# A trunk layer in fp32 on one core: second tokens turned and weighted by ScalarE before the first products, last stores from two queues

## The chip, the core and the metric

The kernel runs on one core of a Trainium2 chip. A core has TensorE for products (PE in the profile, with PEld for its weight loads), VectorE (DVE), ScalarE (ACT), GpSimd (POOL) and SyncE (SP), which here only starts transfers. Each engine works through its own list of instructions in order, and waits on semaphores for the others. Transfers between the chip's main memory and the core's memory run on 16 DMA engines, which are fed by queues that SP, ACT and POOL fill. The metric is the device time of one execution in microseconds (us).

## What is computed

One decoder layer on 512 tokens of 1024 channels, all in fp32: a first RMSNorm and a wide projection, a convolution branch, gated linear attention, a merge with an output projection, a feed-forward block and a last RMSNorm. The change touches the start and the very end:

```python
u = _rmsnorm(h, norm1_g[l])
proj = u @ w_in[l]
a_glu, q, k, v, r, g_low, gate_a, gate_b = _split_cols(proj)
...
return _rmsnorm(h, final_g)
```

where `_rmsnorm(x, g)` is `x * rsqrt(mean(x*x) + EPS) * g`, over the channels of a token. The first thing the kernel produces is the first half (512 columns) of `v`, and the last is the final norm.

## The kernel before

**Products.** An fp32 product is made of three products in a format with fewer bits: each operand is split into a high part (`whi`, `uh`, or the first of two tiles named `h`) and a low part (`wlo`, `ul`, the second tile `h`), and low x high, high x low and high x high are added up in one bank. ScalarE makes the high part by a cast (L256 for weights, L469 for tokens), VectorE the low part by a subtraction (L259, L470). So a block of weights costs one ScalarE and one VectorE pass over 128x1024 elements, and then serves many products.

**The start.** The 512 tokens are four groups t = 0 to 3 of 128. Tokens arrive with a token in each row, and the products need a channel in each row, so TensorE turns each group by eight 128x128 transposes against an identity (`turn`, L378 to L380), four into each of two banks g = 0 and 1 (channels 0 to 511 and 512 to 1023). The weights of `v`'s first half come in four blocks `w_v` j = 0 to 3 of 256 channels each; block j serves channels k = 2j and 2j+1 (in units of 128).

Groups 0 and 1 don't wait for their norm. Their turned tokens are multiplied by the channel weights `norm1_g` alone (`gained`, L475, one VectorE pass over 512 columns from the bank), split (`split_plain`, L480), and used; the factor of each token is applied to the result when it leaves its bank (`v_done`, L534), and later to the kept tokens (`renormed`, L484). Groups 2 and 3 are normed first: `rms` (L452: two squares with sums on ScalarE, one VectorE instruction, one power on GpSimd), `shrunk` (L462, VectorE), then turned, then weighted and split by `spread_gain` (L382), whose high parts are eight ScalarE instructions over 128 columns each (L389: copy with a scale per row, read from the bank).

The transfers of the start are all issued by SP, in this order: x of group 0, `w_v` block 0, x of group 1, blocks 1 and 2, x of group 2, block 3, x of group 3 in two halves. Until the first tokens are there, TensorE multiplies ones by ones (`raise_clock`, L439): seven times before the first transposes and three times after them.

The start runs under a schedule written by hand (`start`, L422): TensorE, ScalarE, VectorE and SP keep the order in which the code calls them (L542 to L584). What matters here:

- TensorE: transposes of group 0; three warm products; four products of block 0 for group 0 that need no `wlo`; transposes of group 1, g = 0; the two products with `wlo`; transposes of group 1, g = 1; six products of block 0 for group 1, whose first needs the low part of group 1; blocks 1 and 2 for both groups; transposes of group 2; block 3; and so on.
- ScalarE: cast of group 0 g 0; cast of block 0; cast of group 1 g 0; cast of block 1; cast of group 0 g 1; cast of group 1 g 1; cast of block 2; squares of group 2; cast of block 3; squares of group 3 and so on.
- VectorE: weighting and low part of group 0 g 0; low part of block 0; weighting and low part of group 1 g 0; weighting of group 0 g 1; low part of block 1; low part of group 0 g 1; weighting and low part of group 1 g 1; low part of block 2; norm of group 2; low part of block 3.

`v_block(j, *ts, low_last, between)` (L509) issues the six products of block j for each group in `ts`; with `low_last` the two that need `wlo` come last, and `between` is called ahead of them.

**The end.** The last feed-forward product adds to the residual `hres`, and the class `Finish` (L1117) norms each group of tokens. For the last group, `store` (L1147) scales columns 0 to 383 on ScalarE (L1152) and columns 384 to 1023 on VectorE (L1155), and sends each part by its own transfer. Both transfers are issued by SP: L1157 (640 columns) and L1154 (384 columns). Three engines keep their written order there (`END`).

Of the kernel before, what the change touches and what calls it, by code (L numbers as in the profile page):

```python
# [14 lines left out]
AF = mybir.ActivationFunctionType  # L15
ALU = mybir.AluOpType

P = 128
D = 1024
T = 512  # L20
NT = T // P
KT = D // P
# [45 lines left out]
def trunk_layer(ctx: ExitStack, tc: tile.TileContext, a: dict, out: bass.AP):  # L68
    nc = tc.nc
# [23 lines left out]
    def nm(s):  # L93
        return f"{s}_{next(names)}"

    def heap(dt=F32):
        return hp.tile([P, T], dt, tag="h", name=nm("h"))
# [13 lines left out]
    def mm_bank():  # L111
        return ps.tile([P, T], F32, tag="mm", name=nm("mm"), bufs=5)

    def ax_bank():
        return ps.tile([P, T], F32, tag="ax", name=nm("ax"), bufs=3)
# [8 lines left out]
    gains = cp.tile([P, 2 * KT], F32, name="gains")  # L124
# [143 lines left out]
    def weight(name, j, ahead=LOOK):  # L268
        assert order[used[0]] == (name, j)
        prefetch(1)  # L270
        used[0] += 1
        prefetch(ahead)
        fill(RATE)
        return ready[used[0] - 1]
# [22 lines left out]
    def mm3(acc, l, r, first, last, more=False):  # L297

        (lh, ll), (rh, rl) = l, r
        kw = {"skip_group_check": True} if more else {}  # L300
        nc.tensor.matmul(acc, ll, rh, start=first, stop=False, **kw)  # L301
        nc.tensor.matmul(acc, lh, rl, start=False, stop=False, **kw)  # L302
        nc.tensor.matmul(acc, lh, rh, start=False, stop=last, **kw)  # L303
# [74 lines left out]
    def turn(x, banks, g):  # L378
        for k in range(4):
            nc.tensor.transpose(banks[g][:, k * P : (k + 1) * P], x[g][:, k * P : (k + 1) * P], ident)  # L380
# [29 lines left out]
    xs = {}  # L410
# [11 lines left out]
    start = tc.manual_schedule(engines=START)  # L422
# [21 lines left out]
    banks = {0: [ax_bank(), ax_bank()]}  # L444
# [7 lines left out]
    def rms(t):  # L452
        ss = small(2, "ss")
        for j in range(2):
            nc.scalar.activation(junk(T), xs[t][j], AF.Square, scale=1.0 / 32.0, accum_out=ss[:, j : j + 1])
        v = small(1, "var")
        nc.vector.scalar_tensor_tensor(v, ss[:, 0:1], EPS, ss[:, 1:2], ALU.add, ALU.add)
        return rsqrt(v, 1)
# [7 lines left out]
    unscaled = {}  # L466

    def split_by(f, hi, lo):
        nc.scalar.copy(hi, f)  # L469
        nc.vector.tensor_tensor(lo, f, hi.bitcast(F32), ALU.subtract)  # L470

    def by_token(x):
        return x.rearrange("p (k t) -> p k t", t=P)

    def gained(t, g):  # L475
        f = unscaled[t, g] = heap()
        gain = gains[:, g * 4 : g * 4 + 4].unsqueeze(2).to_broadcast([P, 4, P])
        nc.vector.tensor_tensor(by_token(f), by_token(banks[t][g]), gain, ALU.mult)

    def split_plain(t, g):  # L480
        plain[t, g] = (heap(F32R), heap(F32R))
        split_by(unscaled[t, g], *plain[t, g])
# [14 lines left out]
    def tokens(t):  # L497
        def normed(k):
            return tuple(x[:, t * P : (t + 1) * P] for x in acts1[k])

        return normed

    def as_landed(t):
        return lambda k: tuple(x[:, k % 4 * P : (k % 4 + 1) * P] for x in plain[t, k // 4])

    accs = [mm_bank() for _ in range(NT)]
    ws = []

    def v_block(j, *ts, low_last=False, between=None):  # L509
        for t in ts:  # L510
            src = as_landed(t) if t < 2 else tokens(t)
            last = []
            for i in range(2):
                k = 2 * j + i
                c = slice(i * T, (i + 1) * T)
                w = (ws[j][0][:, c], ws[j][1][:, c])
                if low_last:
                    ah, al = src(k)
                    nc.tensor.matmul(accs[t], al, w[0], start=k == 0, stop=False)
                    nc.tensor.matmul(accs[t], ah, w[0], start=False, stop=False)  # L520
                    last.append((ah, w[1]))
                else:
                    mm3(accs[t], src(k), w, k == 0, k == KT - 1)
            if between:
                between()
            for ah, wl in last:
                nc.tensor.matmul(accs[t], ah, wl, start=False, stop=False)

    def block_ready():
        ws.append(weight("w_v", len(ws), 0))  # L530
# [11 lines left out]
    banks[1] = [ax_bank(), mm_bank()]  # L542
    gained(0, 0)
    split_plain(0, 0)
    block_ready()
    v_block(0, 0, low_last=True, between=lambda: turn(xs[1], banks[1], 0))
    turn(xs[1], banks[1], 1)
    gained(1, 0)
    split_plain(1, 0)
    gained(0, 1)  # L550
    v_block(0, 1)
    block_ready()
    split_plain(0, 1)
    gained(1, 1)
    v_block(1, 0, 1, low_last=True)
    split_plain(1, 1)
    block_ready()
    v_block(2, 0, 1, low_last=True)
    r1[2] = rms(2)
    shrunk(2)  # L560
    banks[2] = turned(xs[2])
# [44 lines left out]
    for k in range(KT):  # L606
# [4 lines left out]
        c = heap()  # L611
# [95 lines left out]
    rows = slice(32, 32 + RANK)  # L707
# [9 lines left out]
    rows = slice(96, 96 + RANK)  # L717
# [374 lines left out]
    def first_of_pair(i, accs):  # L1092

        w = fp.tile([P, 3 * H], F32, tag="w", name=nm("w"), bufs=2)
        glu(i, accs, w[:, :T])
        nc.vector.tensor_tensor(w[:, T:], w[:, :H], w[:, H:T], ALU.subtract)
        y = fsplit(w.rearrange("p (c t) -> p c t", t=H)[:, 0:3:2, :], T, "y")
        return w, {"a11": y(0), "n3": y(1)}
# [18 lines left out]
    class Finish:  # L1117
# [29 lines left out]
        def store(self):  # L1147
            rows = slice(self.t * P, (self.t + 1) * P)
            if self.y:
                cut = T if self.t < NT - 1 else D - SPLIT  # L1150
                lo, hi = self.y[:, :cut], self.y[:, cut:]
                nc.scalar.activation(lo, lo, AF.Copy, scale=self.r)  # L1152
                if self.t == NT - 1:
                    nc.sync.dma_start(out[rows, :cut], lo)  # L1154
                nc.vector.tensor_scalar(hi, hi, self.r, None, ALU.mult)  # L1155
                if self.t == NT - 1:
                    nc.sync.dma_start(out[rows, cut:], hi)  # L1157
                else:
                    nc.sync.dma_start(out[rows, :], self.y)
                return  # L1160
            for n, y in reversed(self.parts):
                nc.scalar.activation(y, y, AF.Copy, scale=self.r)
                nc.sync.dma_start(out[rows, n * T : (n + 1) * T], y)
# [22 lines left out]
    for gi, pairs in enumerate(GROUPS):  # L1186
        acts = []
        early = {}
        if gi == 0:

            ws = [weight("w_up", j, 0) for i in pairs[0] for j in (i, FT + i)]
            accs = [mm_bank() for _ in ws]
# [7 lines left out]
        def both(i):  # L1200
            return early.get(i) or [col_tile(weight("w_up", i), acts2), col_tile(weight("w_up", FT + i), acts2)]

        for p, q in pairs:
            w, found = first_of_pair(p, both(p))
# [95 lines left out]
```

## Time and profile before

| | |
|---|---|
| time before, median of 3 runs | 841.06 us (840.03 to 841.2) |
| time of the profiled execution | 841.11 us |
| its span from first to last instruction | 839.4 us |
| TensorE's granted clock over the span | 0.997 |
| PE, DVE, ACT, POOL busy | 827.9, 649.8, 398.1, 41.8 us |

The profile has a page with shares and groups of instructions, and a trace that can be asked for more: instructions in order of time, waits (who waited for whom, in total, how often, and the longest), busy time in chosen stretches, and transfers with their time from issue to landing. A row of the timeline reads: start, duration, engine, line, operation, output<-inputs, shape, count, and in brackets the idle time before it and what ended it. L12 is line 12 of the kernel before, as printed above.

### The profile page before, as it was taken

How to read it: one execution, taken by the hardware profiler on the slowest of the kernel's cores; microseconds unless marked ns; L12 is line 12 of the kernel's file. 1: busy time of each engine (PE TensorE's matmuls, PEld its weight loads, DVE VectorE, ACT ScalarE, POOL GpSimd, SP SyncE). 2: the span in 40 equal slices, each digit the busy share in tenths (PEclk: the TensorE clock that was granted, in tenths of full speed). 3: DMA queues.
4: the chain of work that ended last, by engine and by line, in shares of the span. 5: the costliest groups of instructions: out<-in, count | busy, mean ns of one | idle time of the engine just before them, and what ended most of it. 6: DMA issues, size and time to landing. Idle time of an engine off the chain costs nothing.

```text
span 839.4 us, 10105 instructions
## 1 busy us (share of the span) xinstructions
PE 827.9 (99%) x3841; PEld 690.7 (82%) x3841; DVE 649.8 (77%) x954; ACT 398.1 (47%) x590; POOL 41.8 (5%) x64
## 2 busy tenths in 40 slices
PE   8999999999999999999999999999999999999996
PEld 6888888888888888888888898888888888888885
DVE  5779879999997798744687758778757777677795
ACT  5723337535443422449434766444434443444454
POOL 1000000000100100000001000000100010000111
PEclk9999999999999999999999999999999999999998
DMA  7333232222322322222346643335742249222462
GB/s 286 110 102 104 90 105 80 97 101 76 101 76 76 126 90 89 97 86 91 101 100 183 193 151 126 101 87 115 212 144 85 73 86 285 95 89 98 102 126 100
DMA packets 28465, 97.27 MB, mean 116 GB/s; under 512 B 3232, under 2 KB 3504, under 8 KB 28416
## 3 DMA queue, kind: packets, MB, share of 16 engines
q1 hardware_dynamic: 24928, 84.82, 30.0%
q0 software_dynamic: 3456, 11.80, 8.3%
q8 instruction: 30, 0.49, 0.2%
q14 instruction: 19, 0.16, 0.1%
q10 hardware_dynamic: 32, 0.01, 0.0%
HBM read 94.51 MB, written 2.10 MB: 115 GB/s over the span
## 4 chain that ended last, share of the span: by engine, by line
PE 92%; DVE 3%; ACT 2%; issue 1%; DMA 1%; POOL 0%; SPq 0%; POOLq 0%; DVEq 0%; ACTq 0%
PE mm L301 28%; PE mm L303 28%; PE mm L302 28%; DVE wlo L241 1%; DMA hres<-in_x_dram 1%; PE ax L845 1%; PE ax L380 1%; PE ax L847 1%; PE ax L827 1%; PE ax L303 1%; PE ax L301 1%; PE ax L302 1%; DVE wlo L259 1%; DVE hres L995 1%; PE ax L814 0%
## 5 line engine op out<-in xcount | busy, mean ns | idle before, releaser
L301 PE MATMUL mm<-uh,wlo 128*128 128x512 f32 (+1 forms) x768 | 294.7, 384 | 0.0
L303 PE MATMUL mm<-uh,whi 128*128 128x512 f32 (+1 forms) x768 | 292.2, 380 | 0.0
L302 PE MATMUL mm<-ul,whi 128*128 128x512 f32 (+1 forms) x768 | 292.0, 380 | 0.0
L256 ACT CAST whi<-raw 128x1024 fp32r<-128x1024 f32 x116 | 120.9, 1048 | 126.3 <-PE mm L303 94.8
L259 DVE TENSOR_TENSOR wlo<-raw,whi 128x1024 fp32r<-128x1024 f32 x116 | 141.1, 1219 | 34.8 <-ACT whi L256 34.5
L303 PEld LDWEIGHTS mm<-uh,whi 128*128 128x128 f32 x768 | 144.4, 188 | 27.8
L302 PEld LDWEIGHTS mm<-ul,whi 128*128 128x128 f32 x768 | 144.5, 188 | 27.4
L301 PEld LDWEIGHTS mm<-uh,wlo 128*128 128x128 f32 x768 | 144.5, 188 | 26.9
L604 DVE SCALAR_TENSOR_TENSOR c<-h,pp,c 128x511 f32<-128x511 f32 (+14 forms) x240 | 162.5, 730 | 0.7
L1075 DVE SCALAR_TENSOR_TENSOR tmp<-mm,pp,tmp 128x511 f32<-128x511 f32 x88 | 65.8, 748 | 66.7 <-ACT tmp L1073 65.6
L1073 ACT ACTIVATE tmp<-mm,pp 128x512 f32<-128x512 f32 x44 | 34.3, 779 | 61.5 <-PE mm L303 61.5
L240 ACT CAST whi<-kept 128x1024 fp32r<-128x1024 f32 (+1 forms) x32 | 31.7, 993 | 25.9 <-DVE kept L220 12.2
L241 DVE TENSOR_TENSOR wlo<-kept,whi 128x1024 fp32r<-128x1024 f32 (+1 forms) x32 | 36.7, 1153 | 4.3 <-ACT whi L240 4.1
L995 DVE TENSOR_TENSOR hres<-hres,mm 128x512 f32<-128x512 f32 (+1 forms) x49 | 32.6, 672 | 7.2 <-PE mm L303 3.9
L240 ACT CAST whi<-raw 128x1024 fp32r<-128x1024 f32 (+1 forms) x24 | 23.7, 995 | 17.0 <-PE mm L303 16.9
L241 DVE TENSOR_TENSOR wlo<-raw,whi 128x1024 fp32r<-128x1024 f32 (+1 forms) x24 | 27.3, 1153 | 1.6 <-ACT whi L240 1.6
L302 PE MATMUL mm<-wlo,sh 128*128 128x512 f32 x66 | 25.8, 391 | 0.0
L303 PE MATMUL mm<-whi,sh 128*128 128x512 f32 x66 | 25.7, 390 | 0.0
L301 PE MATMUL mm<-whi,sl 128*128 128x512 f32 x66 | 25.5, 389 | 0.0
L301 PE MATMUL mm<-h,wlo 128*128 128x512 f32 x64 | 25.4, 397 | 0.0
L349 POOL TENSOR_TENSOR rstd<-var,mhalf 128x1 f32<-128x1 f32 (+1 forms) x16 | 13.3, 840 | 241.4 <-DVE var L852 196.6
L303 PE MATMUL mm<-h,whi 128*128 128x512 f32 x64 | 24.9, 390 | 0.0
(253 smaller groups left out, 1148.7 us busy)
## 6 DMA issues: line engine op xcount, KB each, us to landing
raw<-in_w_up_dram SPq DMA_DIRECT2D x44, 512.0 KB, 3.5
raw<-in_w_glu_dram SPq DMA_DIRECT2D x16, 512.0 KB, 3.4
raw<-in_w_down_dram SPq DMA_DIRECT2D x15, 512.0 KB, 3.4
kept<-in_w_down_dram POOLq DMA_DIRECT2D x10, 512.0 KB, 5.5
raw<-in_w_v_dram SPq DMA_DIRECT2D x8, 512.0 KB, 4.0
raw<-in_w_qk_dram SPq DMA_DIRECT2D x8, 512.0 KB, 3.3
raw<-in_w_r_dram SPq DMA_DIRECT2D x8, 512.0 KB, 3.2
raw<-in_w_gb_dram SPq DMA_DIRECT2D x8, 512.0 KB, 3.3
```

What stands on the lines that cost most here:

```text
L240: nc.scalar.copy(hi, raw)
L241: nc.vector.tensor_tensor(lo, raw, hi.bitcast(F32), ALU.subtract)
L256: nc.scalar.copy(hi, raw)
L259: pace[0] = nc.vector.tensor_tensor(lo, raw, hi.bitcast(F32), ALU.subtract)
L301: nc.tensor.matmul(acc, ll, rh, start=first, stop=False, **kw)
L302: nc.tensor.matmul(acc, lh, rl, start=False, stop=False, **kw)
L303: nc.tensor.matmul(acc, lh, rh, start=False, stop=last, **kw)
L349: nc.gpsimd.tensor_tensor(r, v, mhalf[:, :n], ALU.pow)
L604: nc.vector.scalar_tensor_tensor(y[:, s:], c[:, : T - s], w, y[:, s:], ALU.mult, ALU.add)
L995: nc.vector.tensor_tensor(hres[t, n][:, c], hres[t, n][:, c], x[:, c], op)
L1073: nc.scalar.activation(z, acc, AF.Identity, bias=pp[:, PP_FB + m : PP_FB + m + 1], scale=w[2])
L1075: nc.vector.scalar_tensor_tensor(z[:, s:], acc[:, : T - s], w[j], z[:, s:], ALU.mult, ALU.add)
```

## The change

Four things change, and nothing else.

1. The four transposes of group 1, g = 0, stand ahead of all products of block 0 rather than between them.
2. For group 1 the channel weights are applied by ScalarE in four instructions of 128 columns (`gained_by_act`) in place of one VectorE instruction of 512 columns, for g = 0 and for g = 1. On ScalarE, the four for g = 0 stand between the cast of block 0 and the cast of group 1; those for g = 1 stand behind the cast of group 0 g 1.
3. The six products of block 0 for group 1 begin with the four that take the group's high part, and end with the two that take its low part. On VectorE the weighting of group 0 g 1 comes ahead of the low part of group 1 g 0. In blocks 0 to 2 for the other cases the order is low, high with `whi`, then high with `wlo`, each for both channels; block 3 and groups 2 and 3 keep their order.
4. In `store`, the transfer of columns 0 to 383 of the last group is issued by ScalarE rather than by SP.

```diff
+    def gained_by_act(t, g):
+        f = unscaled[t, g] = heap()
+        for k in range(4):
+            c = slice(k * P, (k + 1) * P)
+            nc.scalar.activation(f[:, c], banks[t][g][:, c], AF.Copy, scale=gains[:, g * 4 + k : g * 4 + k + 1])
...
+    LOW_LAST = ((1, 0), (0, 0), (0, 1))
+    HIGH_FIRST = ((0, 0), (0, 1), (1, 0))
+    ALL = ((1, 0), (0, 1), (0, 0))
+
+    def v_block(j, *ts, parts=None):
         for t in ts:
             src = as_landed(t) if t < 2 else tokens(t)
...
+            ks = (2 * j, 2 * j + 1)
+            todo = [(k, p) for p in parts for k in ks] if parts else [(k, p) for k in ks for p in ALL]
+            for n, (k, p) in enumerate(todo):
+                product(t, j, k, src, *p, j == 0 and n == 0, j == KT // 2 - 1 and n == len(todo) - 1)
+
+    def product(t, j, k, src, a_low, w_low, first, last):
+        w = ws[j][w_low][:, (k % 2) * T : (k % 2 + 1) * T]
+        nc.tensor.matmul(accs[t], src(k)[a_low], w, start=first, stop=last)
...
     gained(0, 0)
     split_plain(0, 0)
     block_ready()
-    v_block(0, 0, low_last=True, between=lambda: turn(xs[1], banks[1], 0))
+    turn(xs[1], banks[1], 0)
+    v_block(0, 0, parts=LOW_LAST)
+    gained_by_act(1, 0)
+    gained(0, 1)
+    split_plain(1, 0)
     turn(xs[1], banks[1], 1)
-    gained(1, 0)
-    split_plain(1, 0)
-    gained(0, 1)
-    v_block(0, 1)
+    v_block(0, 1, parts=HIGH_FIRST)
     block_ready()
     split_plain(0, 1)
-    gained(1, 1)
-    v_block(1, 0, 1, low_last=True)
+    gained_by_act(1, 1)
+    v_block(1, 0, 1, parts=LOW_LAST)
     split_plain(1, 1)
     block_ready()
-    v_block(2, 0, 1, low_last=True)
+    v_block(2, 0, 1, parts=LOW_LAST)
...
                 if self.t == NT - 1:
-                    nc.sync.dma_start(out[rows, :cut], lo)
+                    nc.scalar.dma_start(out[rows, :cut], lo)
```

From the transposes of group 2 on, every engine's list holds the same instructions in the same order as before, up to the last store.

More of the change, by code (lines that the diff above doesn't have):

```diff
@@ L507, in trunk_layer @@
     ws = []
-    def v_block(j, *ts, low_last=False, between=None):
+    LOW_LAST = ((1, 0), (0, 0), (0, 1))
+    HIGH_FIRST = ((0, 0), (0, 1), (1, 0))
+    ALL = ((1, 0), (0, 1), (0, 0))
+    def v_block(j, *ts, parts=None):
         for t in ts:
             src = as_landed(t) if t < 2 else tokens(t)
[L512 to L527, printed above, removed]
+            ks = (2 * j, 2 * j + 1)
[5 more added lines that the diff above has]
+        nc.tensor.matmul(accs[t], src(k)[a_low], w, start=first, stop=last)
     def block_ready():
```

## The prediction

> **What bounds the kernel now.** I read the page first, then TensorE's waits, the busy time by stretch, and the timeline of the start and of the end.
>
> ```profile
> span 839.4 us, 10105 instructions
> PE 827.9 (99%) x3841; PEld 690.7 (82%) x3841; DVE 649.8 (77%) x954; ACT 398.1 (47%) x590; POOL 41.8 (5%) x64
> PE 92%; DVE 3%; ACT 2%; issue 1%; DMA 1%; POOL 0%; SPq 0%; POOLq 0%; DVEq 0%; ACTq 0%
> ```
>
> TensorE is busy for 99% of the span and is 92% of the chain of waits, so a change that leaves its products as they are can only win where it waits. The waits (who for whom: us in total, times, longest) and the stretches (length, then busy time of PE first):
>
> ```profile
> PE mm L519 <- ACT whi L256: 1.3, 1, 1.3
> PE mm L301 <- DVE h L470: 1.3, 1, 1.3
> PE ax L380 <- ACT un L400: 0.3, 1, 0.3
> PE ax L302 <- DVE wlo L241: 0.3, 1, 0.3
> ...
> PEld mm L527 <- DVE wlo L259: 0.5, 1, 0.5
> ```
>
> ```profile
> 24.00:430.00 406.00, 406.00 (x1860) 338.23 (x1861) 336.46 (x503) 186.13 (x273) 10.19 (x12) 1.00 0.29 94
> 500.00:830.00 330.00, 330.00 (x1497) 274.68 (x1496) 245.07 (x327) 154.18 (x198) 17.48 (x22) 1.00 0.43 119
> ```
>
> The large waits are two of 1.3 us on lines of the start; between 24 and 430 us and between 500 and 830 us PE has no gap. So the start sets when an unbroken run of products begins, and what is won there should reach the end undiminished. Now the start, in order of time:
>
> ```profile
> 7.04 1.04 ACT L256 CAST whi<-raw 128x1024 fp32r<-128x1024 f32 x1
> 8.11 1.23 DVE L259 TENSOR_TENSOR wlo<-raw,whi 128x1024 fp32r<-128x1024 f32 x1 [0.25 <-ACT whi L256]
> 8.13 0.50 PE L519 MATMUL mm<-whi,h 128*128 128x512 f32 x1 [1.30 <-ACT whi L256]
> 9.18 0.60 PE L380 MATMUL ax<-ident,x 128*128 128x128 f32 x4
> 9.53 0.71 PE L527 MATMUL mm<-wlo,h 128*128 128x512 f32 x2
> 10.08 0.60 PE L380 MATMUL mm<-ident,x 128*128 128x128 f32 x4
> 10.54 0.62 ACT L469 CAST h<-h 128x512 fp32r<-128x512 f32 x1 [2.46 <-DVE h L478]
> 11.06 1.04 ACT L256 CAST whi<-raw 128x1024 fp32r<-128x1024 f32 x1
> 11.94 0.50 PE L301 MATMUL mm<-whi,h 128*128 128x512 f32 x1 [1.26 <-DVE h L470]
> 12.27 0.40 PE L302 MATMUL mm<-wlo,h 128*128 128x512 f32 x1
> ...
> 15.38 1.04 ACT L256 CAST whi<-raw 128x1024 fp32r<-128x1024 f32 x1
> 16.32 0.63 ACT L455 ACTIVATE junk<-x 128x512 bf16<-128x512 f32 x1
> 16.47 0.50 PE L519 MATMUL mm<-whi,h 128*128 128x512 f32 x1
> 17.73 0.73 PE L527 MATMUL mm<-wlo,h 128*128 128x512 f32 x2
> 18.67 0.88 DVE L464 TENSOR_SCALAR x<-x,rstd 128x512 f32<-128x512 f32 x2 [0.68 <-POOL rstd L349]
> 19.46 1.22 DVE L259 TENSOR_TENSOR wlo<-raw,whi 128x1024 fp32r<-128x1024 f32 x1
> 19.69 1.03 PE L380 MATMUL ax<-ident,x 128*128 128x128 f32 x8
> ```
>
> Three holes. At 11.94 PE waits for group 1's low part, which waits for the cast at 10.54, for VectorE's weighting, and for transposes that stood behind four products. At 16.47 it waits for the high part of block 2, at 17.73 for its low part; that cast starts at 15.38 only because ScalarE idled (2.46 us ahead of 10.54) and each cast behind it came late.
>
> **Prices.** A product after a wait takes 0.34 us to the next (11.94 to 12.27), else 0.23 (eight from 17.73 to 19.69, less 0.11 for the restart). Four transposes delay what follows by 0.35 (9.18 to 9.53). ScalarE begins an instruction 0.1 before the end of the one ahead (16.32 against 15.38 + 1.04).
>
> The trace has no ScalarE weighting with an fp32 result; the nearest rows read the same kind of bank with the same scale and write the high format, as the page of groups and as the timeline give it:
>
> ```profile
> L389 ACT ACTIVATE uh<-ax,gains 128x128 fp32r<-128x128 f32 x16 | 4.3, 379 | 0.0
> ...
> 21.53 2.16 ACT L389 ACTIVATE uh<-ax,gains 128x128 fp32r<-128x128 f32 x8
> ```
>
> Eight overlap: (2.16 - 0.38) / 7 = 0.25 from one to the next, so four take 3 x 0.25 + 0.38 = 1.13. That is my price; the upper bound is no overlap, 4 x 0.38 = 1.52, and there is no reason for less than 0.25.
>
> **The new order, step by step.** The moved transposes follow the last warm products, in a time when PE idles, if x of group 1 is there:
>
> ```profile
> 1.71 0.42 SPq L416 DMA_DIRECT2D x<-in_x_dram  x1
> x<-in_x_dram SPq DMA_DIRECT2D x1, 512.0 KB, 5.0
> ...
> 5.99 0.83 PE L441 MATMUL ax<-ones 128*128 128x128 f32 x6
> ```
>
> It lands at 1.71 + 5.0 = 6.71, as the warm products end (6.8). The transposes are done by 7.3, before the 8.13 at which products can start; they cost nothing, and would cost from a landing at 7.7 on.
>
> ScalarE: block 0's cast ends at 8.08. Weightings 7.98 to 9.12, cast of group 1 9.15 to 9.77, cast of block 1 9.68 to 10.72 (11.06 before), cast of group 0 g 1 10.63 to 11.25, weightings 11.16 to 12.30, cast 12.33 to 12.95, cast of block 2 12.86 to 13.90, where it began at 15.38 before: 2.5 us earlier although ScalarE has gained 2.3 us of work, for its waits go. Everything behind it there (squares of group 2, cast of block 3) moves by 2.5 as well, if the data are there; x of group 2, issued after block 2, landed by 10.5:
>
> ```profile
> 3.21 0.47 SPq L416 DMA_DIRECT2D x<-in_x_dram  x1
> x<-in_x_dram SPq DMA_DIRECT2D x1, 512.0 KB, 7.3
> ```
>
> TensorE: four products from 8.13 to 9.18 as before; then `wlo`, ready at 8.11 + 1.23 = 9.34, is a new wait of 0.2 (the transposes used to cover it). Two products 9.39 to 9.96, transposes g 1, and at 10.31 group 1's first product, whose high part has been ready since 9.77. Its low part is needed at 11.3; VectorE, rid of two weightings, makes it from 9.9 to 10.6. Six products end at 11.78, block 1's twelve at 14.52 (`whi` at 10.72, `wlo` at 11.97), block 2's at 17.26: its `whi` comes at 13.90, its `wlo` at 15.2 and is needed at 15.4. Group 2's transposes start at 17.26 rather than 19.69; their tokens are normed by 18.67 - 2.5 + 0.88 = 17.05. Block 3's `wlo` follows at 18.2 and is needed at 18.4.
>
> By holes: 1.6 at group 1's first product (11.94 to 10.31; of it 0.1 for the transposes, since the new wait for `wlo` takes most of their place), and 0.8 for the holes ahead of 16.47 and 17.73 with their restarts: 2.4, as 19.69 - 17.26 says. One more comes back at group 3's transposes, eight of which take 0.12 longer than group 2's, waiting for VectorE's low parts that hang on ScalarE, now 2.5 ahead:
>
> ```profile
> 23.39 1.15 PE L380 MATMUL ax<-ident,h 128*128 128x128 f32 x8
> ```
>
> So the start gives 2.5. The margins behind it are thin: 0.2 for either `wlo`, 0.2 for the normed tokens. What is late next is ScalarE, which now runs without a hole from 7 us to the transposes of group 2; a delay there beyond 0.2 costs PE its full length.
>
> **The end.**
>
> ```profile
> 0.80 0.90 ACTq L426 DMA_DIRECT2D row<-in_norm_g_dram  x2
> ...
> 834.47 0.61 ACT L1152 ACTIVATE y<-y,rstd 128x384 f32<-128x384 f32 x1 [0.93 <-POOL rstd L1145]
> ...
> 835.05 0.33 SPq L1157 DMA_DIRECT2D out_dram<-y  x1
> 835.47 0.38 SPq L1154 DMA_DIRECT2D out_dram<-y  x1
> ...
> 835.95:837.25 1.30, 0.00 (x0) 0.00 (x0) 0.00 (x0) 0.00 (x0) 0.00 (x0) 0.50 0.99 383
> ```
>
> The last store is issued 0.42 after the other; ScalarE could issue it at 835.1. But in the last row (transfers of both, share of the 16 DMA engines 0.99 at 383 GB/s) they move data without a break for 1.3 us: the second store's packets wait for the first's, not for their issue. Nothing is queued behind the issue on ScalarE. I price it at 0; bounds: a gain of 0.42 if the issue decided, a loss of 0.1 if ScalarE issues at 0.45 each (0.90 for two) where SP takes 0.33.
>
> The Trainium skill, "DMA: Bandwidth & Descriptors", section "Issuing engines are not separate DMA queues", speaks against a gain: transfers started by different engines interleave on the same 16 DMA engines, and only the issuing time is saved. By that rule the end gives 0, by the spacing of the issue rows alone 0.42; the share of 0.99 agrees with the rule.
>
> **Sum.** 841.11 (the profiled execution; the median shown is 841.06, 0.05 lower) - 2.5 - 0 = 838.6 us, 0.3% faster. The bounds of the weightings and of the end give 838.2 to 839.4 (next part).
>
> **Rivals.** (a) ScalarE becomes the bound: weightings that don't overlap add 0.39 per four, 0.8 by block 2's cast, which then starts 1.7 earlier rather than 2.5, and PE follows it: 839.4, at the edge of what can be told. For it: no margin over 0.2; against it: the overlapping row. Chance 0.14.
>
> (b) The gain is absorbed later, by something that doesn't move with PE: 841.1. For it: VectorE is busy for 336 of the 406 us to 430. Against it: no gap on PE from 24 to 430 us, and the two later waits, 0.3 each, are for engines that move along. Chance 0.09.
>
> (c) Slower: x of group 1 lands late. PE works in order, so the moved transposes now stand ahead of all products, and the ScalarE chain hangs on them. Each us after 7.7 costs a us; from 10.1 on the 2.5 are eaten. A landing like that of group 2's x (10.5) gives 841.5, one at 12 gives 843. Against it: 6.71 here, third in SP's queue. Chance 0.08.
>
> (d) The end does what its spacing says: another 0.4, 838.2. Chance 0.05.
>
> That the order would not come about is no rival: each engine's list in the built kernel is the one written.
>
> **How the numbers follow.** The forecast has 0.64. A measurement of this kernel tells 0.2%, 1.7 us, from no change. Faster: the forecast, (d) and a third of (a), 0.74; same: the rest of (a) and (b), 0.18; slower: (c), 0.08. The forecast's own range is 837.5 (the lowest run before, 840.03, less 2.5) to 839.1 (a loss of 0.5 at the thin margins); with (a) and some of (b) the range is 837.5 to 840.2.
>
> **What would show it.** Right: the first product still at 8.13; group 1's first product near 10.3; the cast of block 2 near 12.9; group 2's transposes near 17.3; no wait on PE over 0.3 from 8.13 to 24 us; the whole timeline then earlier by 2.5 until the last product. Right at the end: the stores' packets stop about 2 us after the issue, as before. Wrong: a first product after 8.2 (c); a wait of PE for `whi` or for normed tokens with ScalarE never idle (a); a shift that shrinks between 24 and 830 us (b).

## The result, and the profile after

| | before | after |
|---|---|---|
| median of 7 runs, us | 841.06 | 838.64 |
| lowest to highest, us | 840.03 to 842.17 | 838.28 to 839.13 |
| profiled execution, us | 841.11 | 838.75 |
| its span, us | 839.4 | 837.0 |
| mean granted TensorE clock in it | 0.997 | 0.997 |

The ratio of after to before is 0.9974, with a 95% interval of 0.9962 to 0.9985. The time came out where it was forecast, 838.6. The terms did not: the start gave 1.75 us and not 2.5, and another 0.65 came from behind it, most of it at a place that the change doesn't touch.

The page of after: the span, each engine's busy time, and the shares of the chain that ended last.

```profile
span 837.0 us, 10108 instructions
PE 827.7 (99%) x3841; PEld 691.3 (83%) x3841; DVE 648.8 (78%) x952; ACT 400.0 (48%) x598; POOL 41.7 (5%) x64
PE 90%; issue 3%; DVE 2%; DMA 2%; ACT 2%; POOL 0%; SPq 0%; POOLq 0%; ACTq 0%; DVEq 0%
```

TensorE's work is the same (827.7 us against 827.9), so the 2.4 us by which the span is shorter were waits. The waits of TensorE's products in after, over the whole span (who for whom: us in total, times, longest; a weight load that waits, PEld, shows in the timeline):

```profile
PE ax L441 <- DVE ones L408: 1.1, 1, 1.1
PE ax L380 <- DMA x<-in_x_dram: 0.7, 1, 0.7
PE ax L380 <- ACT un L400: 0.3, 1, 0.3
```

The two waits of 1.3 us at the start are gone. One of 0.7 us is new: the moved transposes wait for x of group 1. A wait of 0.3 for `wlo` (L241) is gone as well; that line works in the stage of the output projection, near 454 us. First the start, in order of time:

```profile
8.10 0.63 PE L380 MATMUL ax<-ident,x 128*128 128x128 f32 x4 [0.69 <-DMA x<-in_x_dram]
...
8.49 1.17 PE L529 MATMUL mm<-whi,h 128*128 128x512 f32 x4
8.77 1.15 ACT L484 ACTIVATE h<-ax,gains 128x128 f32<-128x128 f32 x4 [0.69 <-PE ax L380]
...
9.39 0.30 PEld L529 LDWEIGHTS mm<-wlo,h 128*128 128x128 f32 x2 [0.17 <-DVE wlo L259]
...
10.62 0.30 PEld L529 LDWEIGHTS mm<-whi,h 128*128 128x128 f32 x2 [0.30 <-ACT h L469]
...
11.94 1.13 ACT L484 ACTIVATE h<-mm,gains 128x128 f32<-128x128 f32 x4
...
13.63 1.05 ACT L256 CAST whi<-raw 128x1024 fp32r<-128x1024 f32 x1
...
15.99 0.30 PEld L529 LDWEIGHTS mm<-wlo,h 128*128 128x128 f32 x2 [0.46 <-DVE wlo L259]
...
17.95 1.04 PE L380 MATMUL ax<-ident,x 128*128 128x128 f32 x8
...
21.61 1.17 PE L380 MATMUL ax<-ident,h 128*128 128x128 f32 x8
...
22.54 0.48 PE L529 MATMUL mm<-whi,ul 128*128 128x512 f32 x1
```

The view of transfers of the same execution gives x of group 1 its time from issue (again at 1.71) to landing:

```profile
x<-in_x_dram SPq DMA_DIRECT2D x1, 512.0 KB, 6.3
```

It lands at 8.0, where the profile of before had 6.71. The first product starts 0.36 late for it (8.49, not 8.13), and ScalarE, which can't weight what isn't turned, starts at 8.77. From there the chain of weightings and casts runs without a hole, and everything behind it is later than forecast by about as much: block 2's cast at 13.63, its low part so late that a weight load waits for 0.46 at 15.99 (the products lose 0.21 there: 1.12 us from 14.87 for four that took 0.91 from 13.50), group 2's transposes at 17.95. The same product then stands 1.75 us earlier than before: 22.54 against this row of before's timeline:

```profile
24.29 0.48 PE L301 MATMUL mm<-whi,ul 128*128 128x512 f32 x1
```

The 1.75 holds for over 400 us. It grows mainly at one place. Timeline of before, where the output projection meets the residual, and the residual's transfers:

```profile
452.37 0.69 DVE L995 TENSOR_TENSOR hres<-hres,mm 128x512 f32<-128x512 f32 x1 [3.16 <-DMA hres<-in_x_dram]
...
454.86 0.50 PE L302 MATMUL ax<-wlo,h 128*128 128x512 f32 x1 [0.27 <-DVE wlo L241]
...
hres<-in_x_dram SPq DMA_DIRECT2D x8, 256.0 KB, 8.2
```

and the same of after:

```profile
449.76 0.69 DVE L998 TENSOR_TENSOR hres<-hres,mm 128x512 f32<-128x512 f32 x1 [2.27 <-DMA hres<-in_x_dram]
...
452.70 0.39 PE L302 MATMUL ax<-wlo,h 128*128 128x512 f32 x1
...
hres<-in_x_dram SPq DMA_DIRECT2D x8, 256.0 KB, 7.6
```

In before, VectorE waited 3.16 us for the residual, came late to `wlo`, and TensorE stood. In after it waited 2.27, and TensorE went on. The shift is 1.72 one product ahead of this one (454.20 and 452.48), 2.16 at it, 2.3 a few products on (457.50 and 455.19) and 2.4 in the spans. Last the end, from after's timeline and its stretch of full transfers:

```profile
832.59 0.33 SPq L1160 DMA_DIRECT2D out_dram<-y  x1
832.65 0.38 ACTq L1157 DMA_DIRECT2D out_dram<-y  x1
...
833.50:834.80 1.30, 0.00 (x0) 0.00 (x0) 0.00 (x0) 0.00 (x0) 0.00 (x0) 0.50 0.99 384
```

The stores are issued 0.06 us apart instead of 0.42, yet the packets still fill the DMA engines (0.99) for 1.3 us, and from the first issue to the end of the span it takes 4.41 us (837.0 - 832.59) against 4.35 before (839.4 - 835.05).

### The profile page after: what moved, and what is told of

Its sections match the earlier page's. It is cut to its first block, busy times and chain, and to the rows that moved or that the text cites. A ratio compares the mean times of both kernels' runs of the same rounds, so it can differ in the third digit from the quotient of the medians.

```text
span 837.0 us, 10108 instructions
## 1 busy us (share of the span) xinstructions
PE 827.7 (99%) x3841; PEld 691.3 (83%) x3841; DVE 648.8 (78%) x952; ACT 400.0 (48%) x598; POOL 41.7 (5%) x64
## 3 DMA queue, kind: packets, MB, share of 16 engines
q0 software_dynamic: 3456, 11.80, 8.3%
## 4 chain that ended last, share of the span: by engine, by line
PE 90%; issue 3%; DVE 2%; DMA 2%; ACT 2%; POOL 0%; SPq 0%; POOLq 0%; ACTq 0%; DVEq 0%
PE mm L301 27%; PE mm L303 27%; PE mm L302 27%; PE mm L529 3%; DMA raw<-in_w_down_dram 1%; PE ax L848 1%; DVE hres L998 1%; DMA x<-in_x_dram 1%; PE ax L850 1%; PE ax L830 1%; PE ax L301 1%; PE ax L303 1%; PE ax L302 1%; PE ax L380 1%; ACT whi L240 0%
## 5 line engine op out<-in xcount | busy, mean ns | idle before, releaser
L241 DVE TENSOR_TENSOR wlo<-kept,whi 128x1024 fp32r<-128x1024 f32 (+1 forms) x32 | 36.7, 1153 | 4.3 <-ACT whi L240 4.1
L241 DVE TENSOR_TENSOR wlo<-raw,whi 128x1024 fp32r<-128x1024 f32 (+1 forms) x24 | 27.3, 1153 | 1.9 <-ACT whi L240 1.8
L349 POOL TENSOR_TENSOR rstd<-var,mhalf 128x1 f32<-128x1 f32 (+1 forms) x16 | 13.3, 839 | 239.9 <-DVE var L855 196.6
```

Source lines behind the costliest of these rows:

```text
L241: nc.vector.tensor_tensor(lo, raw, hi.bitcast(F32), ALU.subtract)
```

## The experiments

Three questions were open: whether x of group 1 regularly lands late; whether the 0.65 us near 454 us belong to the change or to one execution of before; and which part of the edit earns what. Each kernel ran beside before on the same chip; its ratio is to those runs. Line numbers differ by a few between the kernels. One operation of GpSimd near 195 us moves a single execution by some 1.5 or 6.0 us (last section), so small differences between two ratios say little about the start; the traces say more.

### Store or start

The new store alone, put into before:

```diff
-                    nc.sync.dma_start(out[rows, :cut], lo)
+                    nc.scalar.dma_start(out[rows, :cut], lo)
```

> The kernel before with its last store of 384 columns issued by ScalarE, and nothing else. Theory (the 16 DMA engines, not the issue, set the end): within 0.1 us of the kernel before, with the stores' packets again moving for 1.3 us without a break from about 0.9 us after the first issue. Rival (the 0.42 us between the two issues decide): 0.4 us faster. Its start is that of before, so it is also a second look at two things: x of group 1 landing near 6.7 us, and TensorE waiting 0.3 to 0.4 us near 454 us, where VectorE waits for the residual's transfers. Theory A: that second wait comes and goes from run to run with the traffic. Theory B: it belongs to the old start, and is there again.

Measured: 841.89 us (840.16 to 842.81), before 842.11 there; ratio 0.9996 (0.9988 to 1.0005). The store is worth nothing that can be measured. Its trace has the old start and no wait of TensorE near 454 us.

The new start alone, which is after with the store put back on SP:

```diff
-                    nc.scalar.dma_start(out[rows, :cut], lo)
+                    nc.sync.dma_start(out[rows, :cut], lo)
```

> The changed kernel with both last stores issued by SP again. Theory: as fast as the changed kernel, 2.4 us faster than before; rival: 0.4 us less. A second look at the landing of x of group 1: at 6.7 us (then the first product is at 8.13, group 2's transposes near 17.3, and the gain at 24 us 2.4 to 2.5), or at 8.0 as in the first trace of the changed kernel (then 8.5, 17.95 and 1.75). Near 454 us: theory A, TensorE's wait there may come back; theory B, it stays away, and another 0.6 us is won there.

Measured: 838.86 us (838.19 to 840.42), ratio 0.9963 (0.9951 to 0.9976). The whole gain is the start's. Here x of group 1 took 5.9 us to land, and the start ran 0.35 us ahead of after's:

```profile
7.76 0.63 PE L380 MATMUL ax<-ident,x 128*128 128x128 f32 x4 [0.26 <-DMA x<-in_x_dram]
...
17.59 1.03 PE L380 MATMUL ax<-ident,x 128*128 128x128 f32 x8
```

### The parts of the start

The four transposes of group 1 back between the fourth and the fifth product, all else as in after:

```diff
-    turn(xs[1], banks[1], 0)
-    v_block(0, 0, parts=LOW_LAST)
+    v_block(0, 0, parts=LOW_LAST, between=lambda: turn(xs[1], banks[1], 0))
```

> The changed kernel with the first four transposes of group 1 back between the fourth and the fifth product of block 0. Theory (their place decides when ScalarE can begin its weighting: 9.6 us rather than 8.0 to 8.8): group 1's first product near 11.4, block 2's cast near 14.5, group 2's transposes near 18.7, 0.75 to 1.4 us over the changed kernel. Rival (the place is worth only what it covers on TensorE): 0.1 to 0.2 us over it.

Measured: 841.31 us (839.32 to 842.4), ratio 0.9986 (0.9977 to 0.9995). Timeline:

```profile
9.96 1.14 ACT L484 ACTIVATE h<-ax,gains 128x128 f32<-128x128 f32 x4 [1.74 <-PE ax L380]
...
11.80 0.73 PE L531 MATMUL mm<-whi,h 128*128 128x512 f32 x2 [0.98 <-ACT h L469]
...
19.14 1.03 PE L380 MATMUL ax<-ident,x 128*128 128x128 f32 x8
```

ScalarE idles 1.74 us ahead of the weighting, TensorE waits at 11.80, and group 2's transposes are 1.55 us later than in the new start alone (17.59), 1.19 later than in after. By these traces most of the start's gain hangs on the place of the transposes.

Both weightings back on VectorE, all else as in after:

```diff
-    gained_by_act(1, 0)
+    gained(1, 0)
...
-    gained_by_act(1, 1)
+    gained(1, 1)
```

> The changed kernel with both weightings of group 1 on VectorE again, one instruction each, at the same places in the code. Theory (VectorE is kept by the low part of block 0 until 9.3 us, so the weighting ends near 10, the casts behind it are late, and block 2's cast begins near 14.5): group 2's transposes near 18.8, 0.9 to 1.3 us over the changed kernel. Rival (a weighting on VectorE is shorter, 0.69 against 1.13, and ScalarE has none to spare): as fast, or up to 0.3 us faster.

Measured: 840.12 us (839.31 to 844.33), ratio 0.9977 (0.9965 to 0.999). Timeline:

```profile
14.56 1.04 ACT L256 CAST whi<-raw 128x1024 fp32r<-128x1024 f32 x1
...
15.65 1.20 PE L529 MATMUL mm<-whi,h 128*128 128x512 f32 x4 [0.62 <-ACT whi L256]
...
18.87 1.03 PE L380 MATMUL ax<-ident,x 128*128 128x128 f32 x8
```

ScalarE, with less to do, casts block 2 at 14.56, 0.93 later than in after: it waits 1.89 and 1.97 us for VectorE's weightings ahead of its casts at 9.97 and 14.03, and group 2's transposes are 1.28 behind the new start alone and 0.92 behind after. That the work was moved to ScalarE pays because ScalarE is then its own supplier. The two parts don't add up: 1.55 and 1.28 are together more than the 2.1 by which the new start alone is ahead of before (24.29 and 22.18 for the product quoted above), and 1.19 and 0.92 together more than the 1.75 of after, since without either of them the chain through ScalarE is late.

The high products of block 0 for group 1 no longer first:

```diff
-    v_block(0, 1, parts=HIGH_FIRST)
+    v_block(0, 1)
```

> The changed kernel with the six products of block 0 for group 1 in the old order, the one with the low part first. Theory: group 1's first product waits for its low part, 0.3 us (x of group 1 there at 6.7) to 0.7 us (at 8.0) later than in the changed kernel; of that the wait for block 2's low part behind it gives back up to 0.4, so group 2's transposes come 0.3 us later, and so does the end. Rival (every us of a wait in the start reaches the end): 0.7 us.

Measured: 839.02 us (838.25 to 841.47), ratio 0.9966 (0.9953 to 0.9979), not to be told from the new start alone. Its timeline shows the wait that the order avoids, and what is left of it later:

```profile
10.93 0.50 PE L529 MATMUL mm<-whi,h 128*128 128x512 f32 x1 [0.40 <-DVE h L470]
...
17.86 1.03 PE L380 MATMUL ax<-ident,x 128*128 128x128 f32 x8
```

Some 0.3 us at the transposes (17.86 against 17.59) and 0.1 at the product quoted above (22.27 against 22.18), too little for the median.

### x of group 1, later

Its transfer issued behind blocks 1 and 2 of the weights, all else as in after:

```diff
-    load_x(1)
     load()
     load()
+    load_x(1)
```

> The changed kernel with x of group 1 issued two transfers later, behind blocks 1 and 2 of the weights. By the rows of the other transfers it then lands near 9.3 us. Theory (TensorE in its order and ScalarE's chain both hang on that landing): first product near 9.7, group 2's transposes near 18.9 rather than 17.3 to 17.95, the time 1.0 to 1.6 us over the changed kernel's. Rival (the landing is hidden, and the casts of the weights set the pace): within 0.3 us of the changed kernel.

Measured: 842.79 us (840.65 to 846.17), ratio 1.0013 (1.0001 to 1.0026). The gain is gone, as the rival of a late landing had it. Timeline, and then the busy time by stretch (length; PE, PEld, DVE, ACT, POOL; granted clock; share and GB/s of the DMA engines):

```profile
10.36 1.09 PE L380 MATMUL ax<-ident,x 128*128 128x128 f32 x4 [3.29 <-DMA x<-in_x_dram]
...
11.10 2.06 PE L529 MATMUL mm<-whi,h 128*128 128x512 f32 x4
```

```profile
8.00:10.00 2.00, 0.00 (x0) 0.00 (x0) 1.76 (x2) 0.21 (x1) 0.00 (x0) 0.84 1.04 420
10.00:12.00 2.00, 1.64 (x6) 1.57 (x7) 0.07 (x1) 0.51 (x2) 0.00 (x0) 0.50 0.97 373
...
14.00:16.00 2.00, 2.00 (x9) 1.71 (x8) 1.74 (x2) 1.84 (x6) 0.00 (x0) 0.50 0.31 128
16.00:18.00 2.00, 2.00 (x10) 1.67 (x9) 1.10 (x3) 1.97 (x4) 0.00 (x0) 0.95 0.75 248
```

TensorE idles for 3.29 us, and the granted clock falls to 0.50 and stays there until about 16 us. So a late landing costs more than its own length: group 2's transposes come at 22.22, 4.63 behind the new start alone, for transposes of group 1 that are 2.60 later (10.36 against 7.76). The expectation missed both: x landed about 1 us later than it said, and it didn't count the clock. The Trainium skill, "TensorE: Matmul & The Clock Gate", "Part 1: The HAM clock gate", has the array drop to half rate after at least one idle window of about 3.4 us and come back after at least one busy window of that length. The half rate agrees with the 0.50; here it was back some 6 us after work resumed.

### Versions meant to be faster

The weighting of group 1's second half on VectorE, ahead of block 1's low part, so that ScalarE has less:

```diff
+    gained(1, 1)
     block_ready()
     split_plain(0, 1)
-    gained_by_act(1, 1)
```

> The changed kernel with only the second weighting (g = 1) of group 1 on VectorE, ahead of the low part of block 1. Theory (ScalarE's unbroken chain is what is late next): block 2's cast begins 1 us earlier, near 12.0 to 12.6; TensorE has no wait left before group 2's transposes, at 17.3 to 17.5; 0.1 to 0.5 us faster than the changed kernel. Rival (TensorE's own products are the bound, or VectorE becomes it): the same, or slower by up to 0.3.

Measured: 840.25 us (838.74 to 843.2), ratio 0.9975 (0.9961 to 0.9989). Block 2 is cast at 12.28, 1.0 before the new start alone, and no weight load waits for its low part any more. Timeline:

```profile
11.03 0.68 DVE L478 TENSOR_TENSOR h<-mm,gains 128x512 f32<-128x512 f32 x1
11.63 1.21 DVE L259 TENSOR_TENSOR wlo<-raw,whi 128x1024 fp32r<-128x1024 f32 x1
...
12.28 1.05 ACT L256 CAST whi<-raw 128x1024 fp32r<-128x1024 f32 x1
...
12.90 0.30 PEld L529 LDWEIGHTS mm<-wlo,h 128*128 128x128 f32 x2 [0.33 <-DVE wlo L259]
...
17.57 1.03 PE L380 MATMUL ax<-ident,x 128*128 128x128 f32 x8
```

But the weighting at 11.03 now stands ahead of block 1's low part, and a weight load waits for that, 0.33 us at 12.90: a wait has moved one block forward. Group 2's transposes are where they were, though x of group 1 was 0.17 later in this trace (transposes at 7.93 against 7.76), and the product quoted above is 0.2 earlier (21.98 against 22.18). So the start may be a little better; the times don't show it.

x of group 1 issued second, ahead of block 0, with VectorE's weightings and the products of block 0 for both groups mixed:

```diff
-    load()
     load_x(1)
     load()
     load()
+    load()
...
+    v_block(0, 0, parts=LOW_LAST[:2])
+    v_block(0, 1, parts=HIGH_FIRST[:1])
+    v_block(0, 0, parts=LOW_LAST[2:], opens=False)
+    v_block(0, 1, parts=HIGH_FIRST[1:], opens=False)
```

> A version meant to beat both: x of group 1 is issued second, ahead of block 0; both weightings of group 1 are VectorE's, the first one ahead of block 0's low part; the two products of group 1's high part with block 0 stand between the four and the two of group 0, so that they cover the wait for block 0's low part; the squares of group 2 come ahead of the last cast of group 1. Theory (landing of x, ScalarE's chain and the wait for the low part were what kept TensorE): no wait over 0.2 us after the first product, group 2's transposes near 17.1, 0.5 to 0.8 us faster than the changed kernel. Rival (block 0, now third, lands late instead, or VectorE, with two weightings more, is late with block 0's low part): the same or slower.

Measured: 839.21 us (838.0 to 841.0), ratio 0.9959 (0.9946 to 0.9972). Now block 0 is the third transfer, and late:

```profile
8.06 1.04 ACT L256 CAST whi<-raw 128x1024 fp32r<-128x1024 f32 x1 [0.93 <-DMA raw<-in_w_v_dram]
...
9.16 1.65 PE L529 MATMUL mm<-whi,h 128*128 128x512 f32 x6 [0.92 <-ACT whi L256]
```

Group 2's transposes start at 17.95, as late as in after, where 17.1 was expected. The ratio is the lowest of the study, but its interval overlaps those of the new start alone and of the old order of products; it isn't shown to be faster.

Two more keep the transfers' order, let ScalarE cast block 0 before the first tokens, do four products ahead of group 1's transposes, weight on VectorE and square group 2 ahead of the last cast of group 1; the second of them takes x of group 1 in two halves (the last piece of the edit):

```diff
-    split_plain(0, 0)
     block_ready()
+    split_plain(0, 0)
+    v_block(0, 0, parts=HIGH_FIRST[:2])
     turn(xs[1], banks[1], 0)
-    v_block(0, 0, parts=LOW_LAST)
-    gained_by_act(1, 0)
+    v_block(0, 0, parts=HIGH_FIRST[2:], opens=False)
+    gained(1, 0)
...
-            nc.sync.dma_start(x, a["x"][t * P : (t + 1) * P, :])
+            for j in range(2 if t == 1 else 0):
+                nc.sync.dma_start(xs[t][j], a["x"][t * P : (t + 1) * P, j * T : (j + 1) * T])
+            if t != 1:
+                nc.sync.dma_start(x, a["x"][t * P : (t + 1) * P, :])
```

They ran with after itself on one chip:

> A version meant to beat both: ScalarE casts block 0 (landed by 5.4 us) ahead of group 0's tokens, VectorE makes its low part before theirs; group 0's products begin with the high part, and group 1's transposes stand behind the first four of them, at the time at which x of group 1 lands; both weightings are VectorE's. Theory (the order of ScalarE's first casts set 8.13, and the landing of the third transfer what followed): first product near 7.2, group 1's first near 10.1, group 2's transposes 17.0 to 17.3, 0.4 to 0.8 us under the changed kernel. Rival (block 1's landing, 8.1 to 9.3, and ScalarE behind it are the bound all the same): within 0.3 us of the changed kernel.

> The same with x of group 1 loaded as two transfers of 512 columns, the first of which is all that the first four transposes need. Theory: the first half lands 0.5 us earlier than the whole did, the transposes need not wait, another 0 to 0.3 us. Rival: rows of 2 KB instead of 4 KB, and one issue more, make the transfers behind it later by as much.

> The changed kernel itself once more, on the chip of the two runs below, for a comparison in pairs. Its third transfer (x of group 1) landed 5.8 to 6.3 us after its issue in nine of ten traces so far, and 5.0 in the one that the prediction was read from. If that is the rule, it lands at 7.5 to 8.0 again: first product 8.1 to 8.5, group 2's transposes 17.6 to 17.95, the time 2.0 to 3.0 us under the kernel before, of it 1.7 to 2.1 by 24 us of the trace. If the 5.0 comes back, group 2's transposes are near 17.3. In either case no wait on TensorE near 454 us.

| kernel | median, us (range) | ratio to before |
|---|---|---|
| after | 844.05 (839.56 to 844.62) | 0.9983 (0.9963 to 1.0002) |
| block 0 cast first | 842.9 (840.02 to 845.26) | 0.9976 (0.9957 to 0.9995) |
| the same, x of group 1 in halves | 843.37 (839.39 to 845.02) | 0.9983 (0.9961 to 1.0004) |

Before had 844.87 (840.57 to 847.56) on this chip. No order among the three can be told, and after itself is not clear of no change here. The first product comes early (7.01) in the second row's kernel, but TensorE waits 0.5 us for ScalarE's cast of tokens ahead of it and as long again at 10.35, and group 2's transposes start at 17.34, where after itself had them at 17.27 in its trace on this chip; the halves gave nothing either (17.51).

## Why the prediction was right, and where it wasn't

**The landing of x of group 1: the step that failed.** "It lands at 1.71 + 5.0 = 6.71 ... they cost nothing" read one execution, and that one was the exception. The same transfer, third in SP's queue, took 5.5 to 6.3 us in the traces of after and of every experiment that leaves it third and whole. The prediction's own sign of rival (c), a first product after 8.2, is there (8.49). The bound of 7.7 for a free landing was wrong too: it asked when TensorE would need the transposes, but the step itself let ScalarE weight from 7.98 on. In after the weighting starts 0.67 behind the transposes (8.77 and 8.10), so transposes that start after about 7.3 (7.98 - 0.67) delay the chain. Three executions with the same start show the price, start of group 1's transposes against group 2's: 8.10 and 17.95 in after, 7.76 and 17.59 in the new start alone, and in after's second trace:

```profile
7.40 0.63 PE L380 MATMUL ax<-ident,x 128*128 128x128 f32 x4 [0.88 <-DMA x<-in_x_dram]
...
8.06 1.14 ACT L484 ACTIVATE h<-ax,gains 128x128 f32<-128x128 f32 x4 [0.26 <-PE ax L380]
```

with group 2's at 17.27. One for one: from the second trace to the first, 0.7 us later at the one, 0.68 at the other. That 17.27 is the prediction's 17.26 is luck: x of group 0 was early there (block 0's cast at 6.76, in after at 7.04), and ScalarE waited for the transposes in this trace as well, as the row at 8.06 shows. In all three traces group 2's transposes start 9.16 to 9.21 us behind ScalarE's first weighting (8.06, 8.43, 8.77), and in none of them was the landing free. Rival (c) was thus present in the result with 0.7 us, where its own threshold of 7.7 would have charged 0.3 for a landing at 8.0; taken further (transposes at 10.36) it takes the whole gain, and its price of one for one is too low there, because TensorE's clock falls.

**The weightings on ScalarE.** The price of 1.13 for four was right (1.15 and 1.13), so rival (a) in its form of weightings that don't overlap is out. Its picture of the margin was right: ScalarE, 0.79 late (8.77 for 7.98), cost TensorE nearly its full length: block 2's cast came at 13.63 for 12.86, the wait at 15.99 is for `wlo`, not for the tokens, and group 2's transposes came 0.69 late.

**The new wait for `wlo`** is hidden in after, where the first product is late: a weight load waits 0.17, but the fifth product comes 1.00 behind the first (8.49 to 9.49), no more than the 1.05 of before. In the new start alone (8.35 to 9.61) and in after's second trace (7.86 to 9.12) it is 1.26, so there the wait has its price of 0.2. Group 1's first product, forecast for 10.31, came at 10.62, held by the late cast. The 0.1 that group 3's transposes were to give back didn't come: 0.93 us from 21.61 to 22.54, 0.90 before (23.39 to 24.29); in the old order of products it did (0.79, 21.48 to 22.27). The start gave 1.75.

**"What is won there should reach the end undiminished"** held from 24 to 450 us, so rival (b) fell. Then 0.65 was added. The prediction had quoted before's wait for `wlo` of L241 and not asked whether every execution has it. TensorE's products wait there in 2 of the 13 traces, before's and the one with x issued second; VectorE's wait for the residual was 3.16 and 3.31 us in these two. Where it was 2.65 to 3.04 (five traces, all with a new start), a weight load alone waits there, 0.2 to 0.6 us, the longer the later the residual; where it was 1.98 to 2.27 (six traces, one of them with the old start, store alone), nothing does. The wait therefore comes and goes with VectorE's wait for the residual, and isn't tied to the old start. What lengthens that in one execution stays open: the median time of the eight transfers doesn't tell it (8.2 in before, but also in the new store alone). Nor does every lead reach the end: in the new start alone a product at 700.48 us comes 0.48 behind the one ahead of it (700.00) instead of 0.23, which after's trace doesn't have.

**The end.** Priced at 0, measured 0.9996 (0.9988 to 1.0005); rival (d), 0.4 us or 0.05%, is not supported by the time from the first issue to the end, though the interval alone would still hold it: 4.35 and 4.33 us in the two traces with both stores on SP (before and the new start alone), 4.31 to 4.47 in the eleven with ScalarE's. The unchanged share of 0.99 agrees with the Trainium skill, "DMA: Bandwidth & Descriptors", "Issuing engines are not separate DMA queues": transfers started by different engines run on the same 16 DMA engines.

So the forecast was right in kind (the start alone pays, by shorter waits of one chain through ScalarE) and its size was met partly by luck: a start worth 1.75 in that trace and a gain of 0.65, most of it from the one execution of before, which waited at 454 us. Whether before's other runs waited there isn't known. By the product quoted above the start is worth 1.75 in after, 2.11 in the new start alone and 2.43 in after's second trace, with x of group 0 0.2 later and 0.3 earlier in the last two (block 0's cast at 7.25 and 6.76); 2.5 was seen in none.

## What to carry to other kernels

Moving work ahead of a wait makes its inputs' landing the new bound: take that landing from several executions, and compare it with the first engine of the chain that needs it (here ScalarE, for which the transposes had to start by 7.3 us), not only with the engine that is the bottleneck. A step can be better placed on the engine that consumes its result next, even at a higher price (four instructions of together 1.13 us here for one of 0.69). A difference between two single traces is searched along the whole span for places that the change doesn't touch before it is credited to the change.

## What the hardware showed that was not expected

One small operation of GpSimd has several durations. Its powers at L349 near 195 us, two in a row, in the timelines of before, of the new store alone and of after's second trace:

```profile
195.41 1.78 POOL L349 TENSOR_TENSOR rstd<-var,mhalf 128x2 f32<-128x2 f32 x2 [114.06 <-DVE var L852]
```

```profile
195.25 4.80 POOL L349 TENSOR_TENSOR rstd<-var,mhalf 128x2 f32<-128x2 f32 x2 [114.07 <-DVE var L852]
...
200.61 1.13 PE L862 MATMUL ax<-ident,o 128*128 128x128 f32 x6 [1.08 <-ACT o L856]
```

```profile
193.02 6.65 POOL L349 TENSOR_TENSOR rstd<-var,mhalf 128x2 f32<-128x2 f32 x2 [114.06 <-DVE var L855]
```

The same instructions on the same data take 1.78, 4.80 or 6.65 us. In the middle case TensorE waits for 1.08 us and loses some 1.5 in all: the new store alone is 0.16 ahead of before at these transposes (199.16 and 199.32) and 1.37 behind at the products `ax<-h,kt` (214.77 and 213.40). In the last it waits for 2.5 us, and the stretches behind that wait show more of the price:

```profile
198.00:200.00 2.00, 0.43 (x2) 0.25 (x2) 1.11 (x2) 0.96 (x3) 1.67 (x2) 0.82 0.28 55
200.00:202.00 2.00, 2.00 (x9) 1.64 (x9) 0.75 (x1) 2.00 (x4) 0.00 (x0) 0.50 0.54 207
```

The clock is halved within a wait of 2.5 us, less than the 3.4 us that the Trainium skill's page (above) gives. This trace is 2.43 ahead of before at 24 us (21.86 and 24.29) and 3.58 behind at `ax<-h,kt` (216.98 and 213.40): 6.0 us, more than twice what the change gains, and that execution took 844.39 us. The short form stands in six of the thirteen traces (five kernels with the new start, and before), a longer one in seven, old and new start alike. The times of one kernel spread accordingly (the old order of products: 838.25 to 839.07 seven times, 840.37 to 841.47 five times), which is why ratios, taken side by side on one chip, are used here rather than times from different chips. That this operation makes the spread is inferred from one trace per kernel, and it isn't all of it: the trace with x in halves has the form of 4.80 us and is, with 839.59, one of its kernel's fastest runs. VectorE beside it runs the same instructions at the same distances in before and in the new store alone, so that doesn't tell the forms apart; what lengthens the operation wasn't tried.
